# A maximum over rows on Trainium2: a first load of two rows from its own contiguous megabyte, with its own store, and the last two rows in alternating pieces

## The chip, the cores and the metric

One core of one Trainium2 chip. The metric is the device time of one execution in microseconds (us), lower is better. "Span" is the time from the first to the last instruction in the profile of one execution; the time is a little longer than the span. A transfer "lands" when the last of the 16 DMA engines has reported its share done.

## The reference

```python
batch, seq, dim = 32, 512, 1024
x = np.random.randn(batch, seq, dim).astype(np.float32)     # 67.11 MB
out = np.max(x, axis=-1)                                     # 16384 floats, 64 KB
```

x is 16384 rows of 1024 floats. The kernel treats it as 128 partitions of 128 rows. Below, "a row" is one row in each of the 128 partitions, so 512 KB; a load of 15 rows is 7.86 MB.

## The kernel before

The 128 rows are divided in blocks. In a block of S rows, partition p takes rows p*S to p*S+S-1 of the block, so each load brings a contiguous run per partition, and the results of a partition are S neighbouring floats of the output. Loads go through a ring of 46 rows. VectorE reduces each load; a few parts of late rows are reduced elsewhere (TensorE transposes, ScalarE copies, GpSimd reduces over partitions, TensorE turns the result back, VectorE merges). At the end the results of the two blocks are stored: the first block as 128 runs of 112 floats (448 bytes), in three stores, the second as 128 runs of 16 floats (64 bytes).

```python
BLOCKS = [
    [15, 15, 15, 14, 12, 11, 9, 8, 7, 6],     # 112 rows
    [4, 3, 2, 2, 1, 1, 1],                    # 14 rows, and two more in pieces
]
RING = 46
...
for sizes in BLOCKS:
    S = sum(sizes) + 2 * (sizes is BLOCKS[-1])
    xb = xf[first * P:(first + S) * P, :].rearrange("(p i) d -> p i d", p=P)
    dst = bass.AP(tensor=of.tensor, offset=of.offset + first * P, ap=[[S, P], [1, S]])
    views.append((dst, res[:, first:first + S]))
...                                           # loads and reduces
piece = ring[:, at, :D - K]                   # 689 columns of the last row but one
nc.sync.dma_start(out=piece, in_=xb[:, S - 2, :D - K])
...                                           # 671 columns across both rows, 688 of the last
for p, q in ((0, 48), (48, 96), (96, P)):
    store = nc.scalar.dma_start(out=views[0][0][p:q], in_=views[0][1][p:q])
    tc.add_manual_dep(store.ins, latest_row.ins.name, SYNC, reason="behind the loads")
nc.scalar.dma_start(out=views[1][0], in_=views[1][1])
```

## Time and profile before

| | before |
|---|---|
| time, median of 4 runs | 164.04 us (163.95 to 164.29) |
| span of the profiled run | 162.3 us |
| time less span | 1.8 us |
| load queue | 67.11 MB, 96.7% of the 16 engines' span |
| VectorE busy | 135.4 us, 83% |

The 15-row loads land at an even 1.209 us a row, the smaller ones at nearly that, and what follows the last landing is a reduce and a store. The list of DMA issues of the last microseconds (columns: number of issues, KB of each, median us from issue to landing):

```profile
out_dram<-res ACTq DMA_DIRECT2D x2, 21.0 KB, 1.5
out_dram<-res ACTq DMA_DIRECT2D x1, 14.0 KB, 1.5
out_dram<-res ACTq DMA_DIRECT2D x1, 8.0 KB, 1.4
```

### The profile page before, as it was taken

How to read it: one execution, taken by the hardware profiler on the slowest of the kernel's cores; microseconds unless marked ns; L12 is line 12 of the kernel's file. 1: busy time of each engine (PE TensorE's matmuls, PEld its weight loads, DVE VectorE, ACT ScalarE, POOL GpSimd, SP SyncE). 2: the span in 40 equal slices, each digit the busy share in tenths (PEclk: the TensorE clock that was granted, in tenths of full speed). 3: DMA queues.
4: the chain of work that ended last, by engine and by line, in shares of the span. 5: the costliest groups of instructions: out<-in, count | busy, mean ns of one | idle time of the engine just before them, and what ended most of it. 6: DMA issues, size and time to landing. Idle time of an engine off the chain costs nothing.

```text
span 162.3 us, 305 instructions
## 1 busy us (share of the span) xinstructions
PE 14.0 (9%) x76; PEld 12.0 (7%) x76; DVE 135.4 (83%) x35; ACT 6.3 (4%) x8; POOL 16.2 (10%) x11
## 2 busy tenths in 40 slices
PE   0000000000000000000000000000003010736540
PEld 0000000000000000000000000000002010725440
DVE  3000079995999779998999999999999999999994
ACT  3000000000000000000000000000001000222020
POOL 0000000000000000000000000000000500095970
DMA  7999699988999699999998998999999999999990
GB/s 242 485 485 454 273 485 485 485 379 348 485 485 485 285 410 452 452 452 388 497 472 371 433 455 355 436 436 420 509 396 445 452 395 396 440 411 423 405 379 18
DMA packets 3200, 67.18 MB, mean 414 GB/s; under 512 B 640, under 2 KB 640, under 8 KB 1408
## 3 DMA queue, kind: packets, MB, share of 16 engines
q1 hardware_dynamic: 2880, 67.11, 96.7%
q10 hardware_dynamic: 320, 0.07, 0.2%
HBM read 67.11 MB, written 0.07 MB: 414 GB/s over the span
## 4 chain that ended last, share of the span: by engine, by line
DVE 57%; DMA 36%; issue 5%; DVEq 0%
DVE res L168 52%; DMA ring<-in_x_dram 36%; DVE fetched L168 5%; DVEq L249 0%
## 5 line engine op out<-in xcount | busy, mean ns | idle before, releaser
L168 DVE TENSOR_REDUCE res<-ring 128x15 f32<-128x15360 f32 (+10 forms) x15 | 124.1, 8302 | 23.7 <-DMA ring<-in_x_dram 23.7
L143 POOL PARTITION_ALL_REDUCE top<-sb x7 | 16.0, 2330 | 141.8 <-ACT sb L141 141.8
L135 PE MATMUL ps<-ident,ring 128*128 128x128 f32 x38 | 9.3, 425 | 133.8 <-DMA ring<-in_x_dram 133.8
L135 PEld LDWEIGHTS ps<-ident,ring 128*128 128x128 f32 x38 | 7.5, 223 | 134.1 <-issue 127.8
L141 ACT COPY sb<-ps 128x768 f32<-128x768 f32 (+3 forms) x7 | 5.1, 739 | 150.2 <-PE ps L135 150.2
L168 DVE TENSOR_REDUCE fetched<-ring 128x2 f32<-128x1280 f32 (+3 forms) x5 | 8.5, 1699 | 0.0
L161 PE MATMUL fetched<-ident,top 1*128 1x1 f32 x38 | 4.8, 243 | 10.8 <-DVE fetched L168 7.3
L161 PEld LDWEIGHTS fetched<-ident,top 1*128 1x128 f32 x38 | 4.5, 213 | 12.5 <-issue 8.0
L168 DVE TENSOR_REDUCE res<-res 128x2 f32<-128x672 f32 (+1 forms) x2 | 1.7, 858 | 0.0
L141 ACT ACT_TABLE_LOAD x1 | 1.3, 1283 | 0.7 <-PEq L238 0.7
L83 DVE MEMSET ident<- 128x128 f32 x1 | 0.2, 165 | 0.8 <-PEq L238 0.8
L168 DVE TENSOR_REDUCE res<-fetched 128x2 f32<-128x8 f32 (+3 forms) x5 | 0.7, 158 | 0.0
L90 DVE TENSOR_SCALAR rowno<-rowno 32x1 f32<-32x1 f32 x3 | 0.4, 146 | 0.1
L85 DVE TENSOR_TENSOR_SCAN colno<-ident 128x128 f32<-128x128 f32 x1 | 0.4, 425 | 0.0
L92 DVE TENSOR_SCALAR ident<-colno,rowno 128x128 f32<-128x128 f32 x1 | 0.3, 285 | 0.0
L87 DVE STREAM_TRANSPOSE rowno<-colno 128x32 f32<-128x32 f32 x1 | 0.2, 213 | 0.0
L238 POOL MEMSET const-float32-0.0<- 128x1 f32 x1 | 0.1, 98 | 0.2 <-issue 0.2
L238 POOL MEMSET const-bfloat16-1.0<- 128x1 bf16 x1 | 0.1, 101 | 0.0
L238 POOL MEMSET const-uint8-127<- 128x1 uint8 x1 | 0.1, 101 | 0.0
L238 POOL MEMSET const-float32-1.0<- 128x1 f32 x1 | 0.1, 99 | 0.0
L84 DVE MEMSET rowno<- 128x32 f32 x1 | 0.1, 85 | 0.0
## 6 DMA issues: line engine op xcount, KB each, us to landing
ring<-in_x_dram SPq DMA_DIRECT2D x3, 7680.0 KB, 38.4
ring<-in_x_dram SPq DMA_DIRECT2D x1, 7168.0 KB, 37.0
ring<-in_x_dram SPq DMA_DIRECT2D x1, 6144.0 KB, 33.4
ring<-in_x_dram SPq DMA_DIRECT2D x1, 5632.0 KB, 28.6
ring<-in_x_dram SPq DMA_DIRECT2D x1, 4608.0 KB, 39.1
ring<-in_x_dram SPq DMA_DIRECT2D x1, 4096.0 KB, 33.3
ring<-in_x_dram SPq DMA_DIRECT2D x1, 3584.0 KB, 29.0
ring<-in_x_dram SPq DMA_DIRECT2D x1, 3072.0 KB, 35.9
```

The lines of the kernel that those rows point to most:

```text
L83: in_turn("DVE", nc.vector.memset(ident, 1.0))
L84: in_turn("DVE", nc.vector.memset(rowno, 0.0))
L85: in_turn("DVE", nc.vector.tensor_tensor_scan(out=colno, data0=ident, data1=ident, initial=-1.0, op0=ALU.add, op1=ALU.mult))
L87: in_turn("DVE", nc.vector.transpose(out=rowno, in_=colno[:, :32]))
L90: in_turn("DVE", nc.vector.tensor_scalar(out=part, in0=part, scalar1=float(q * 32), scalar2=None, op0=ALU.add))
L92: in_turn("DVE", nc.vector.tensor_scalar(out=ident, in0=colno, scalar1=rowno[:, 0:1], scalar2=None, op0=ALU.is_equal))
L135: in_turn("PE", nc.tensor.transpose(out=ps[:, k * P:(k + 1) * P], in_=rows(j)[:, loads[j][1] - m + r + i, c0 * P:(c0 + 1) * P], identity=i ...
L141: in_turn("ACT", nc.scalar.copy(out=sb[:, :W], in_=ps[:, :W]))
L143: in_turn("POOL", nc.gpsimd.partition_all_reduce(top[:, :W], sb[:, :W], P, bass_isa.ReduceOp.max))
L161: in_turn("PE", nc.tensor.transpose(out=share(j)[:, c0, r + i:r + i + 1], in_=tops[j, c][0:1, k * P:(k + 1) * P], identity=ident[0:1, 0:1],))
L168: return in_turn("DVE", nc.vector.reduce_max(out=out, in_=in_, axis=X))
L238: nc = _bacc.Bacc("TRN2", target_bir_lowering=False, num_devices=1)
```

## The change

The intent: VectorE should not wait 18.9 us for its first load, so the first load has 2 rows only. They are a block of their own, so that load reads one contiguous megabyte; a block has its own store. The last two rows come in four pieces in turn (first part of each row, then the rest), so the last reduce is shorter, and merges stand later in VectorE's order. The diff, cut to its core:

```diff
 BLOCKS = [
-    [15, 15, 15, 14, 12, 11, 9, 8, 7, 6],
-    [4, 3, 2, 2, 1, 1, 1],
+    [2],
+    [15, 9, 15, 14, 12, 10, 9, 9, 8, 6, 5],
+    [4, 3, 2, 1, 1, 1],
 ]
-RING = 46
-SHARED = {7: (2, 3), 9: (4, 4), 11: (3, 3), 13: (2, 3), 16: (1, 1)}
+RING = 47
+SHARED = {9: (1, 4), 10: (2, 4), 11: (2, 4), 12: (3, 2), 13: (2, 3), 14: (2, 3), 17: (1, 2)}
+PIECES = [(604, 420), (568, 456)]
+PLAN = """
+    d0 d1 d2 d3 d4 d5 d6 d7 d8 d9 t0 t1 p9 d10 b0 p10 t2 m9 d11 b1 p11 m10 d12 t3 p12 b2 m11
+    d13 t4 p13 b3 t5 p14 m12 d15 b4 d16 m13 p17 t6 f0 b5 f1 f2 b6 m14 f3 m17
+""".split()
...
-    ring = once.tile([P, RING, D], F32)
-    res = once.tile([P, MID + D - W], F32)
+    ring = once.tile([P, I + RING * D], F32)
+    res = ring[:, :I]
...
-    for p, q in ((0, 48), (48, 96), (96, P)):
-        store = nc.scalar.dma_start(out=views[0][0][p:q], in_=views[0][1][p:q])
-        tc.add_manual_dep(store.ins, latest_row.ins.name, SYNC, reason="behind the loads")
-    nc.scalar.dma_start(out=views[1][0], in_=views[1][1])
+    for dst, src in views[:-1]:
+        store = nc.scalar.dma_start(out=dst, in_=src)
+        tc.add_manual_dep(store.ins, behind.ins.name, SYNC, reason="behind the loads")
+    nc.scalar.dma_start(out=views[-1][0], in_=views[-1][1])
```

In PLAN, d is a direct reduce of a load, p the part of a shared load that VectorE keeps, t and b the way to the other engines and back, m a merge, f a reduce of a piece. The stores are now 128 runs of 2 floats (8 bytes), of 112 floats (448 bytes), and of 14 floats (56 bytes).

More of the change, by code (lines that the diff above doesn't have):

```diff
@@ L13 @@
 BLOCKS = [
-    [15, 15, 15, 14, 12, 11, 9, 8, 7, 6],
-    [4, 3, 2, 2, 1, 1, 1],
-]
-RING = 46
-SHARED = {7: (2, 3), 9: (4, 4), 11: (3, 3), 13: (2, 3), 16: (1, 1)}
-TENSOR = [
-    ("turn", 7, 0), ("back", 7, 0), ("turn", 9, 0), ("turn", 9, 1),
-    ("back", 9, 0), ("turn", 11, 0), ("turn", 11, 1), ("back", 9, 1),
-    ("turn", 13, 0), ("back", 11, 0), ("back", 11, 1), ("turn", 16, 0),
-    ("back", 13, 0), ("back", 16, 0),
-]
-MERGE = {8: (7,), 12: (9,), 15: (11,), 18: (13, 16)}
+    [2],
+    [15, 9, 15, 14, 12, 10, 9, 9, 8, 6, 5],
+    [4, 3, 2, 1, 1, 1],
+]
+RING = 47
[5 more added lines that the diff above has]
+""".split()
 NOSYNC = mybir.DependencyInfo(mybir.DependencyClass.NoSync, mybir.DependencyReason.DATA)
@@ L48 @@
     N, D = xf.shape
-    H = D // 2
     C = D // P
@@ L58 @@
     psmall = ctx.enter_context(tc.tile_pool(name="psmall", bufs=4, space=bass.MemoryType.PSUM))
-    ring = once.tile([P, RING, D], F32)
-    W = 336
-    K = W - 1
-    AT = I + 16
-    MID = AT + K + W + 17
-    res = once.tile([P, MID + D - W], F32)
+    ring = once.tile([P, I + RING * D], F32)
+    res = ring[:, :I]
     latest = {}
@@ L76, in in_turn, with maximum @@
         return inst
+    def maximum(out, in_):
+        return in_turn("DVE", nc.vector.reduce_max(out=out, in_=in_, axis=X))
     ident = once.tile([P, P], F32)
@@ L91 @@
             out=part, in0=part, scalar1=float(q * 32), scalar2=None, op0=ALU.add))
-    in_turn("DVE", nc.vector.tensor_scalar(
+    identity = in_turn("DVE", nc.vector.tensor_scalar(
         out=ident, in0=colno, scalar1=rowno[:, 0:1], scalar2=None, op0=ALU.is_equal))
     loads = []
+    views = []
+    last = len(PIECES)
     first = at = 0
-    views = []
     for sizes in BLOCKS:
-        S = sum(sizes) + 2 * (sizes is BLOCKS[-1])
+        S = sum(sizes) + last * (sizes is BLOCKS[-1])
         xb = xf[first * P:(first + S) * P, :].rearrange("(p i) d -> p i d", p=P)
@@ L111, with share, turn @@
     assert first == I
-    def chunks(j):
-        m, parts = SHARED[j]
+    shared = [SHARED.get(j, (0, C)) for j in range(len(loads))]
+    chunks = []
+    for j, (m, parts) in enumerate(shared):
         per = max(1, C // parts)
-        return [(r, min(per, m - r)) for r in range(0, m, per)]
+        chunks += [(j, r, min(per, m - r)) for r in range(0, m, per)]
     def rows(j):
         start, n, _, _ = loads[j]
-        return ring[:, start:start + n, :]
+        return ring[:, I + start * D:I + (start + n) * D].rearrange("p (i d) -> p i d", d=D)
     tops = {}
-    backs = {}
-    def turn(j, c):
-        m, parts = SHARED[j]
-        r, q = chunks(j)[c]
+    fetched = {}
+    def share(j):
+        m, parts = shared[j]
+        if j not in fetched:
+            got = psmall.tile([P, parts + (parts < C), m], F32)
+            fetched[j] = got
+        return fetched[j]
+    def turn(k):
+        j, r, q = chunks[k]
+        m, parts = shared[j]
         W = q * parts * P
@@ L132, in turn @@
         for i in range(q):
-            for c0 in range(parts):
-                k = i * parts + c0
+            for c in range(parts):
+                w = (i * parts + c) * P
                 in_turn("PE", nc.tensor.transpose(
-                    out=ps[:, k * P:(k + 1) * P],
-                    in_=rows(j)[:, loads[j][1] - m + r + i, c0 * P:(c0 + 1) * P],
+                    out=ps[:, w:w + P],
+                    in_=rows(j)[:, loads[j][1] - m + r + i, c * P:(c + 1) * P],
                     identity=ident,
@@ L144, in turn, with back @@
             top[:, :W], sb[:, :W], P, bass_isa.ReduceOp.max))
-        tops[j, c] = top
-    def share(j):
-        m, parts = SHARED[j]
-        if j not in backs:
-            fetched = psmall.tile([P, parts + (parts < C), m], F32)
-            backs[j] = fetched
-        return backs[j]
-    def back(j, c):
-        m, parts = SHARED[j]
-        r, q = chunks(j)[c]
+        tops[k] = top
+    def back(k):
+        j, r, q = chunks[k]
+        parts = shared[j][1]
         for i in range(q):
-            for c0 in range(parts):
-                k = i * parts + c0
+            for c in range(parts):
+                w = (i * parts + c) * P
@@ L161, in back @@
                 in_turn("PE", nc.tensor.transpose(
-                    out=share(j)[:, c0, r + i:r + i + 1],
-                    in_=tops[j, c][0:1, k * P:(k + 1) * P],
+                    out=share(j)[:, c, r + i:r + i + 1],
+                    in_=tops[k][0:1, w:w + P],
                     identity=ident[0:1, 0:1],
                 ))
-    def maximum(out, in_):
-        return in_turn("DVE", nc.vector.reduce_max(out=out, in_=in_, axis=X))
-    def merge(j):
-        for i in MERGE.get(j, ()):
-            _, k, _, c0 = loads[i]
-            q, _ = SHARED[i]
-            maximum(res[:, c0 + k - q:c0 + k], share(i).rearrange("p k m -> p m k"))
@@ L177, with direct, partial @@
-    issued = done = 0
-    todo = list(TENSOR)
-    for j in range(len(loads)):
-        while issued < len(loads) and issued < j + 3:
+    def direct(j):
+        _, n, _, col = loads[j]
+        k = n - shared[j][0]
+        maximum(res[:, col:col + k], rows(j)[:, :k, :])
+    def partial(j):
+        m, parts = shared[j]
+        maximum(share(j)[:, parts, :], rows(j)[:, loads[j][1] - m:, parts * P:])
+    def merge(j):
+        _, n, _, col = loads[j]
+        maximum(res[:, col + n - shared[j][0]:col + n], share(j).rearrange("p k m -> p m k"))
@@ new lines @@
+    at = at if at + last + 1 <= RING else 0
+    pieces = []
+    tail = []
+    room = I + at * D
+    for q in range(len(PIECES[0])):
+        for r, widths in enumerate(PIECES):
+            c, w = sum(widths[:q]), widths[q]
+            room = -(-(room + 1) // 16) * 16
+            pieces.append((ring[:, room:room + w], xb[:, S - last + r, c:c + w]))
+            if q:
+                tail[-last] = (ring[:, room - 1:room], tail[-last][1])
+            tail.append((res[:, I - last + r:I - last + r + 1],
+                         ring[:, room - (q > 0):room + w]))
+            room += w
@@ L181, with issue @@
+    assert room <= I + (at + last + 1) * D
+    readers = [0] * len(loads)
+    for step in PLAN:
+        if step[0] in "dp":
+            readers[int(step[1:])] += 1
+        elif step[0] == "t":
+            readers[chunks[int(step[1:])][0]] += 1
+    issued = 0
+    behind = None
+    def issue():
+        nonlocal issued
+        while issued < len(loads):
             start, n, src, _ = loads[issued]
-            held = any(s < start + n and start < s + k for s, k, _, _ in loads[j:issued])
@@ L183 @@
-            if held:
-                break
-            nc.sync.dma_start(out=rows(issued), in_=src)
+            if any(readers[j] and s < start + n and start < s + k
+                   for j, (s, k, _, _) in enumerate(loads[:issued])):
+                return
+            load = nc.sync.dma_start(out=rows(issued), in_=src)
             issued += 1
-        while todo and todo[0][1] < (j if todo[0][0] == "back" else issued):
-            what, i, c = todo.pop(0)
-            (turn if what == "turn" else back)(i, c)
@@ L190 @@
-        _, n, _, col = loads[j]
-        m, parts = SHARED.get(j, (0, 0))
-        if n > m:
-            maximum(res[:, col:col + n - m], rows(j)[:, :n - m, :])
-        if m and parts < C:
-            maximum(share(j)[:, parts, :], rows(j)[:, n - m:, parts * P:])
-        merge(j)
-    for what, i, c in todo:
-        assert what == "back"
-        back(i, c)
-    if at + 1 > RING:
-        at = 0
-    piece = ring[:, at, :D - K]
-    nc.sync.dma_start(out=piece, in_=xb[:, S - 2, :D - K])
-    pair = xb[:, S - 2:, :].rearrange("p i d -> p (i d)")
@@ L206 @@
-    nc.sync.dma_start(out=res[:, AT:AT + K + W], in_=pair[:, D - K:D + W])
-    nc.sync.dma_start(out=res[:, MID:], in_=pair[:, D + W:])
-    latest_row = maximum(res[:, AT - 1:AT], piece)
-    merge(len(loads))
-    maximum(
-        bass.AP(tensor=res.tensor, offset=res.offset + I - 2,
-                ap=[list(res.ap[0]), [MID - 1 - (I - 2), 2]]),
-        res[:, AT - 1:AT + K + W].rearrange("p (r k) -> p r k", r=2))
-    merge(len(loads) + 1)
-    maximum(res[:, I - 1:I], res[:, MID - 1:])
@@ L220 @@
-    for p, q in ((0, 48), (48, 96), (96, P)):
-        store = nc.scalar.dma_start(out=views[0][0][p:q], in_=views[0][1][p:q])
-        tc.add_manual_dep(store.ins, latest_row.ins.name, SYNC, reason="behind the loads")
-    nc.scalar.dma_start(out=views[1][0], in_=views[1][1])
+        if any(readers[j] and s < at + last + 1 and at < s + k for j, (s, k, _, _) in enumerate(loads)):
+            return
+        while pieces:
+            nc.sync.dma_start(out=pieces[0][0], in_=pieces[0][1])
+            pieces.pop(0)
@@ new lines @@
+    for step in PLAN:
+        issue()
+        kind, k = step[0], int(step[1:])
+        if kind in "dp":
+            (direct if kind == "d" else partial)(k)
+            readers[k] -= 1
+        elif kind == "t":
+            turn(k)
+            readers[chunks[k][0]] -= 1
+        elif kind == "b":
+            back(k)
+        elif kind == "m":
+            merge(k)
+        else:
+            inst = maximum(*tail[k])
+            if behind is None:
+                behind = inst
+    for dst, src in views[:-1]:
+        store = nc.scalar.dma_start(out=dst, in_=src)
+        tc.add_manual_dep(store.ins, behind.ins.name, SYNC, reason="behind the loads")
```

## The prediction

> **What bounds the kernel now.** I read the page's summary first, then VectorE's timeline, SyncE's timeline and waits, and last the helper engines near the end.
>
> The page (queue, kind: packets, MB, share of 16 engines' span):
>
> ```profile
> DVE  3000079995999779998999999999999999999994
> ...
> q1 hardware_dynamic: 2880, 67.11, 96.7%
> ...
> HBM read 67.11 MB, written 0.07 MB: 414 GB/s over the span
> ```
>
> VectorE is 83% busy but waits for loads; the load queue occupies the 16 engines for 96.7% of the span. 67.11 MB are all of x, and no version can read less. So the load stream is the first candidate, and the question is its pace. VectorE's timeline (start us, us, operation, idle before):
>
> ```profile
> 21.42 16.15 DVE L168 TENSOR_REDUCE res<-ring 128x15 f32<-128x15360 f32 x1 [18.91 <-DMA ring<-in_x_dram]
> 39.55 16.15 DVE L168 TENSOR_REDUCE res<-ring 128x15 f32<-128x15360 f32 x1 [1.98 <-DMA ring<-in_x_dram]
> 57.70 16.16 DVE L168 TENSOR_REDUCE res<-ring 128x15 f32<-128x15360 f32 x1 [1.99 <-DMA ring<-in_x_dram]
> 74.64 55.86 DVE L168 TENSOR_REDUCE res<-ring 128x14 f32<-128x14336 f32 x5 [0.79 <-DMA ring<-in_x_dram]
> ...
> 157.34 0.86 DVE L168 TENSOR_REDUCE res<-ring 128x1 f32<-128x689 f32 x1
> 158.24 0.85 DVE L168 TENSOR_REDUCE res<-res 128x2 f32<-128x672 f32 x1
> 159.01 0.22 DVE L168 TENSOR_REDUCE res<-fetched 128x2 f32<-128x8 f32 x2
> 159.15 0.86 DVE L168 TENSOR_REDUCE res<-res 128x1 f32<-128x689 f32 x1
> ```
>
> Each of the first starts just after its load has landed. 15-row loads (7.864 MB) land 18.13 to 18.15 us apart: 434 GB/s. The reduces take 1.077 us a row against 1.209 us of loading, so VectorE gains 0.13 us on the stream with every row; it loses its slack only because it first waits 18.9 us. From 74.64 on it never idles in this view, so at the end both limits nearly meet. SyncE's timeline shows when the last pieces are issued; its waits say what for:
>
> ```profile
> 138.93 0.33 SPq L204 DMA_DIRECT2D ring<-in_x_dram  x1
> 143.82 0.33 SPq L206 DMA_DIRECT2D res<-in_x_dram  x1
> 147.52 0.33 SPq L207 DMA_DIRECT2D res<-in_x_dram  x1
> ```
>
> ```profile
> SPq L204 <- DMA ring<-in_x_dram: 7.0, 1, 7.0
> SPq L206 <- DMA ring<-in_x_dram: 4.5, 1, 4.5
> SPq L207 <- DMA ring<-in_x_dram: 3.3, 1, 3.3
> ```
>
> Each issue waits for the DMA that used the same of eight completion semaphores before it, here the loads of 6, 4 and 3 rows, so 143.82 and 147.52 are landing times. 4 rows took 4.89 us, 3 rows 3.70, 15 rows 18.14, 14 rows 16.94 (57.70 to 74.64). One line fits all four: **1.204 us a row plus 0.08 us a load**. The piece of line 207 lands 11.5 us after its issue began (the view of DMA issues), at 159.0; the last reduce starts at 159.15. So the bound is the stream, never starved, then a tail of 3.3 us from the last landing to the end of the span (162.3). In the tail are the 0.86 us reduce, the last store, and the end of the program:
>
> ```profile
> 160.04 0.36 ACTq L223 DMA_DIRECT2D out_dram<-res  x1
> ```
>
> This store lands 1.4 us after its issue starts; some 0.9 us of closing waits follow.
>
> **What the Trainium skill says.** "DMA: Bandwidth & Descriptors", section Specifications, gives a fabric ceiling of 435 GB/s into SBUF and about 358 GB/s of HBM for a core. The trace agrees with the first (434 GB/s in the large loads) and exceeds the second; with one core running, 435 is the roof, so 67.11 MB cannot take under 154.3 us (an estimate from that page's figure). The same page, "Why a DMA increments its semaphore by 16 and not by 1", says that only the full count means that all data has landed; so the slowest of 16 engines sets each landing. The trace's landing records agree: for the first load the fifteenth engine reports at 21.14 us and the last at 21.39. "VectorE: DVE Perf Modes", "The perf-mode tier table", gives tensor_reduce no mode above one element a cycle; the trace agrees, 16155 ns for 15360 elements, 1.05 ns each. No page says that a contiguous first megabyte starts faster.
>
> **The change part by part.**
>
> *Small first load.* VectorE's first 18.9 us wait becomes about 3.3: the stream's effective start, 21.42 - 18.14 = 3.28, plus 2 x 1.204 + 0.08 puts the first landing at 5.77. VectorE then does 2.2 us of work and waits again, for the 15 rows, until 3.28 + 2.49 + 18.14 = 23.9. So VectorE is 2 rows ahead of where it would have been, but the stream has the same bytes to move. VectorE's slack is worth nothing unless its lag was the end. It was, by 159.15 - 159.0 = 0.15 us at most.
>
> *Count of loads.* 17 loads and 3 pieces become 18 and 4. One load more: +0.08 us. The old three pieces carry two rows (2 x 1.204 = 2.41 us); the last ordinary load lands at 3.28 + 126 x 1.204 + 17 x 0.08 = 156.34 (the transposes of that row do start at 156.45), so the pieces take 159.0 - 156.34 = 2.7 us, an overhead of 0.1 us each. One piece more: +0.1 us. The last landing moves from about 159.03 to **159.2**.
>
> *Ring.* I walked the new order: load 4 (14 rows) needs loads 0 and 1 reduced, at 40.1, while load 3 streams until about 52; load 5 needs load 2 (49.8) before 69; loads 6 and 7 need load 3 (69.1) before 84; load 9 needs load 5 (97.8) before 118. The last pieces wait for landings of loads 10 to 13 (135.4 to 150.1), with five rows still queued. At each point at least 10 us of data are queued. The stream isn't starved: 0 us.
>
> *The new tail.* Landings by the same line: load 13 at 150.05, 14 at 152.54, 15 to 17 at 153.82, 155.10 and 156.39; the pieces of 604, 568, 420 and 456 columns at 157.21, 157.98, 158.58 and 159.23. VectorE at 1.042 ns an element and 0.06 us from one start to the next: d12 146.4, p12 147.5, m11 149.97, d13 150.07, p13 151.2, p14 152.6, m12 153.98, d15 154.1, d16 155.2, m13 156.33, p17 156.43, f0 157.3, f1 158.0, f2 158.65, m14 159.15, f3 159.25. Every one is within 0.1 to 0.3 us of the landing that it needs: the plan is balanced. f3 reads 457 elements: 0.62 us to its end against 0.86 for 689: **-0.24 us**. But the merge m17 is now behind it, +0.1 us. VectorE ends at **159.95**, against 160.01 before.
>
> *Helpers.* The reductions handed to TensorE, ScalarE and GpSimd grow from 38 to 40 blocks of 128 columns, 0.28 us less for VectorE, already in the walk. The last one, of load 17, is what could be late:
>
> ```profile
> 156.45 0.45 PE L135 MATMUL ps<-ident,ring 128*128 128x128 f32 x1 [1.29 <-DMA ring<-in_x_dram]
> ...
> 157.65 0.95 PE L161 MATMUL fetched<-ident,top 1*128 1x1 f32 x7 [0.76 <-POOL top L143]
> ```
>
> Now two blocks: transposes done near 157.0, copy 157.45, GpSimd free from the one before at about 157.5, some 1.05 us for 256 columns (the earlier 768 took 2.50 us, 384 1.4, 128 0.7), back by 159.0. m17 wants it at 159.8: 0.8 us in hand. "Merges later" protects this; before, no merge made VectorE idle either.
>
> *Stores.* Three stores of the first block become one of 112 columns plus one of 2; both are issued behind f0, at about 158 and 158.5, before the last at 160. They lie beside the last reduces. 0 us.
>
> **Sum:** +0.08 +0.1 in the stream, -0.24 +0.1 in the last reduce and merge, about -0.1 for the lag of 0.15 that is gone: -0.06 us. Span 162.2; the time is 1.8 us above the span now (164.1 to 162.3), so **164.0 us**.
>
> **The rivals.** (1) *The tail slips.* Between the landings of load 17 and of the last piece, 2.84 us, VectorE has 2.8 us of work (p17 to m14). If starts cost 0.1 us instead of 0.06, or a merge waits for GpSimd, the end moves 0.3 to 0.8 us: 164.3 to 164.8. Against it: the old tail ran as tightly. (2) *The stream starts differently.* Data at full pace is reckoned from 3.28 although the first issue is at 0.72; with 8 KB packets from one megabyte this loss could shrink or grow by up to 0.5 us, and the engine that is 0.25 us late could be level: 163.4 to 164.5. The profile has no such start to compare. (3) *VectorE was the bound, and its early start pays.* The unbroken work from 74.64 speaks for it. If true, most of the 2 rows' early work would be a gain, about 2 us: 162. But the last two starts follow landings by 0.12 us, and the roof forbids it. (4) *Starvation:* a wait for a completion semaphore holds the issue long enough to empty the queue; 2 us or more, 166 or more. The walk shows no such place.
>
> **Range and chances.** Rivals 1 and 2 give most of the spread: **163.3 to 164.7**. Faster by over 2% needs 160.8, which would put the last landing at 155.7, a stream above the 434 GB/s seen: 1%. Slower by over 2%, 167.4, needs starvation: 2%. Within 2%: **97%**.
>
> **What would show it.** In the changed profile: first reduce at about 5.8 and the second at 23.9; the last f reduce starts at 159.1 to 159.4 right after its landing; the load queue's share stays at 96 to 97%; span 161.8 to 162.9. Right in mechanism: last landing within 0.3 us of before. It would be wrong if the first landings differ from 5.8 and 23.9 by over 0.5 us, if the loading pace in the middle leaves 1.209 us a row, or if f3 starts over 0.3 us after its landing.

## More of the kernel before

All runs told here were in the undisturbed state.

All four stores of the kernel before land about 1.5 us after their issue.

## The result

The changed kernel took 165.73 us (median of 4 runs, 165.63 to 166.21) against 164.04. The ratio is 1.0106, with a 95% interval of 1.0093 to 1.012. (Every ratio here is from fast runs of the same rounds, and not quite the ratio of the medians.) The output is correct. The rise of 1.7 us is clear of noise and lies outside the predicted range; at 1.1% it is within the 2% that the prediction gave 97%.

The page of the changed kernel, the lines that answer to those of before:

```profile
span 164.0 us, 325 instructions
...
DVE  3500019999992999899999999999999999999990
...
q1 hardware_dynamic: 3168, 67.11, 95.6%
q10 hardware_dynamic: 432, 0.07, 0.2%
```

VectorE now has a little work in the second of the 40 slices, then waits. The same bytes are moved. VectorE's timeline of the changed kernel:

```profile
5.58 2.29 DVE L75 TENSOR_REDUCE ring<-ring 128x2 f32<-128x2048 f32 x1 [3.07 <-DMA ring<-in_x_dram]
23.83 25.81 DVE L75 TENSOR_REDUCE ring<-ring 128x15 f32<-128x15360 f32 x2 [15.96 <-DMA ring<-in_x_dram]
52.89 16.15 DVE L75 TENSOR_REDUCE ring<-ring 128x15 f32<-128x15360 f32 x1 [3.25 <-DMA ring<-in_x_dram]
69.83 48.33 DVE L75 TENSOR_REDUCE ring<-ring 128x14 f32<-128x14336 f32 x4 [0.78 <-DMA ring<-in_x_dram]
...
157.25 1.92 DVE L75 TENSOR_REDUCE ring<-ring 128x1 f32<-128x604 f32 x3
159.09 0.16 DVE L75 TENSOR_REDUCE ring<-got 128x2 f32<-128x8 f32 x1
159.16 0.62 DVE L75 TENSOR_REDUCE ring<-ring 128x1 f32<-128x457 f32 x1
159.70 0.15 DVE L75 TENSOR_REDUCE ring<-got 128x1 f32<-128x3 f32 x1
```

This is the predicted walk within 0.2 us: first reduce 5.58 (5.8 predicted), second 23.83 (23.9), last reduce 159.16 (159.25), end of VectorE 159.85 (159.95). VectorE ends 0.16 us **earlier** than in the kernel before (160.01). And still the span ends 1.7 us later. What lies between is the stores. ScalarE's queue issues them on time:

```profile
158.06 0.86 ACTq L237 DMA_DIRECT2D out_dram<-ring  x2
159.88 0.34 ACTq L239 DMA_DIRECT2D out_dram<-ring  x1
```

But the list of DMA issues of the last microseconds of the changed kernel shows that they land late:

```profile
out_dram<-ring ACTq DMA_DIRECT2D x1, 56.0 KB, 4.5
out_dram<-ring ACTq DMA_DIRECT2D x1, 1.0 KB, 3.9
out_dram<-ring ACTq DMA_DIRECT2D x1, 7.0 KB, 3.2
```

(SyncE's waits at the end of the program don't measure this: its longest wait for a store is 4.1 us here and 0.8 before, but also 4.1 in blocks_3_stores and 5.1 in before_more_loads, two runs told below whose stores all land in 1.4 to 1.5 us.) In the trace's packet records the 8-byte packets of the smallest store are done at 159.13, but its sixteen landing records come in from 159.77 to 162.00. The two other stores land right behind it, 162.15 to 162.94 and 162.72 to 163.12.

There is a second part. The four runs of the changed kernel have spans of 164.0, 163.5, 163.5 and 163.4 us, a mean of 163.6, with times 2.23 us longer than the spans on average. In all runs of the kernel before whose spans are on record, the time is 1.78 us longer than the span on average. So about 0.45 us of the rise do not stand in the span at all.

### The profile page after: what moved, and what is told of

Same layout as the page of the kernel before. It is cut to its first block, busy times and chain, and to the rows that moved or that the text cites. A ratio compares the mean times of both kernels' runs of the same rounds, so it can differ in the third digit from the quotient of the medians.

```text
span 164.0 us, 325 instructions
## 1 busy us (share of the span) xinstructions
PE 15.3 (9%) x80; PEld 12.3 (8%) x80; DVE 135.6 (83%) x42; ACT 6.7 (4%) x8; POOL 17.0 (10%) x11
## 3 DMA queue, kind: packets, MB, share of 16 engines
q1 hardware_dynamic: 3168, 67.11, 95.6%
## 4 chain that ended last, share of the span: by engine, by line
DMA 55%; DVE 40%; issue 2%; SPq 0%; DVEq 0%
DMA ring<-in_x_dram 55%; DVE ring L75 37%; DVE got L75 3%; SPq L210 0%; DVEq L264 0%
## 5 line engine op out<-in xcount | busy, mean ns | idle before, releaser
L75 DVE TENSOR_REDUCE ring<-ring 128x1 f32<-128x1024 f32 (+13 forms) x20 | 125.0, 6281 | 23.3 <-DMA ring<-in_x_dram 23.2
L147 POOL PARTITION_ALL_REDUCE top<-sb x7 | 16.8, 2399 | 141.5 <-ACT sb L145 141.5
L139 PE MATMUL ps<-ident,ring 128*128 128x128 f32 x40 | 10.2, 425 | 142.0 <-DMA ring<-in_x_dram 138.0
L75 DVE TENSOR_REDUCE got<-ring 128x2 f32<-128x1024 f32 (+4 forms) x7 | 9.6, 1371 | 0.0
L157 PE MATMUL got<-ident,top 1*128 1x1 f32 x40 | 5.4, 244 | 1.9 <-POOL top L147 1.9
L157 PEld LDWEIGHTS got<-ident,top 1*128 1x128 f32 x40 | 4.8, 212 | 4.2 <-POOL top L147 3.5
L75 DVE TENSOR_REDUCE ring<-got 128x2 f32<-128x10 f32 (+4 forms) x7 | 1.1, 156 | 0.0
```

The lines of the kernel that those rows point to most:

```text
L75: return in_turn("DVE", nc.vector.reduce_max(out=out, in_=in_, axis=X))
L139: in_turn("PE", nc.tensor.transpose(out=ps[:, w:w + P], in_=rows(j)[:, loads[j][1] - m + r + i, c * P:(c + 1) * P], identity=ident,))
L147: in_turn("POOL", nc.gpsimd.partition_all_reduce(top[:, :W], sb[:, :W], P, bass_isa.ReduceOp.max))
L157: in_turn("PE", nc.tensor.transpose(out=share(j)[:, c, r + i:r + i + 1], in_=tops[k][0:1, w:w + P], identity=ident[0:1, 0:1],))
```

## The experiments

Four theories of the stores were set against each other: (A) the 8-byte store is confirmed late and holds up what lands after it; (B) the last store is slow, as its runs are now 56 bytes and not 64; (C) the one store of 112 columns, formerly three, is slow; and, after the first runs, (D) what counts is whether neighbouring runs share a 64-byte line of memory. For the part outside the span, the rivals are counts of instructions, the number of stores, the place of the results and the size of the ring.

All edits are to the changed kernel ("after") or to the kernel before. Ratios are against runs of the kernel before in the same rounds.

| run | from | time, us | ratio | mean span | time less span |
|---|---|---|---|---|---|
| no_small_store | after | 164.22 | 1.0015 | 162.0 | 2.2 |
| early_small_store | after | 165.83 | 1.0114 | 163.7 | 2.2 |
| early_apart | after | 164.27 | 1.0012 | 162.0 | 2.2 |
| last_2_of_2 | before | 167.23 | 1.0207 | 165.5 | 1.8 |
| last_2_of_8 | before | 165.12 | 1.0052 | 163.3 | 1.8 |
| last_2_of_16 | before | 164.16 | 1.0006 | 162.3 | 1.8 |
| last_14_of_14 | before | 164.59 | 1.0040 | 162.9 | 1.8 |
| last_14_of_16 | before | 164.10 | 1.0005 | 162.3 | 1.8 |
| last_8_of_8 | before | 164.04 | 1.0004 | 162.3 | 1.8 |
| blocks_of_64B | after | 164.32 | 1.0019 | 162.1 | 2.2 |
| blocks_38 | after | 164.57 | 1.0029 | 162.4 | 2.2 |
| blocks_3_stores | after | 164.48 | 1.0015 | 162.4 | 2.2 |
| blocks_own_res | after | 164.30 | 1.0006 | 162.1 | 2.2 |
| blocks_ring46 | after | 164.12 | 1.0009 | 161.9 | 2.2 |
| before_padded | before | 164.05 | 1.0002 | 162.3 | 1.8 |
| before_pe40 | before | 165.00 | 1.0055 | 163.2 | 1.8 |
| before_more_loads | before | 164.36 | 1.0017 | 162.6 | 1.8 |
| before_1_store | before | 164.30 | 1.0005 | 162.5 | 1.8 |

### The small store taken away, or moved

```diff
-    for dst, src in views[:-1]:
+    for dst, src in views[1:-1]:          # no_small_store
```

> The changed kernel without the store of the first block (2 columns, 128 rows of 8 bytes); its 256 results are left unwritten on purpose, so the output is wrong. In the changed profile that store's landing records run from 159.77 to 162.00 us although its packets were done at 159.13, and the two later stores land behind it at 162.94 and 163.12. Theory A (the 8-byte store is confirmed late and holds up what lands after it): the last store lands about 1.4 us after its issue, as before, span about 162.1, time 163.9 to 164.1, 1% under the changed kernel. Theory B (the last store itself is slow, since its rows are now 56 bytes instead of 64): landing of the last store stays near 3.2 us after issue, time 165.4 to 165.8. Theory C (the one store of 112 columns, formerly three, is slow): it still lands over 3 us after issue, time 165 or more.

Measured: 164.22 us, span 162.0. The two remaining stores, of the same shapes as in the changed kernel, land at once:

```profile
out_dram<-ring ACTq DMA_DIRECT2D x1, 56.0 KB, 1.6
out_dram<-ring ACTq DMA_DIRECT2D x1, 7.0 KB, 1.4
```

This settles A against B and C for the changed kernel: the 56-byte runs and the single store of 112 columns are not slow there; they only landed behind the small store. The small store is worth 163.6 - 162.0 = 1.6 us of span. Without it, the rest of the change is 0.2 us **better** in the span than the kernel before (162.23 on average in those rounds).

```diff
             (direct if kind == "d" else partial)(k)
             readers[k] -= 1
+            if step == "d0":                # early_small_store
+                nc.scalar.dma_start(out=views[0][0], in_=views[0][1])
...
-    for dst, src in views[:-1]:
+    for dst, src in views[1:-1]:
```

> The changed kernel with the 2-column store issued as soon as the first reduce is done (about 8 us) instead of at the end. All results correct. Theory A: its slow landing is hidden beside the loads; time 163.9 to 164.2, and its own landing is still 3 us or more after issue. If A is right but the store also delays loads on its engines, the landing of the load after it moves by up to 2 us and the time stays between 164.2 and 165.7. Theories B and C: 165.4 to 165.8, unchanged.

Measured: 165.83 us; nothing was hidden. VectorE's timeline without the small store, first, and with it issued at 8.0 us:

```profile
23.66 25.81 DVE L75 TENSOR_REDUCE ring<-ring 128x15 f32<-128x15360 f32 x2 [15.83 <-DMA ring<-in_x_dram]
52.74 16.15 DVE L75 TENSOR_REDUCE ring<-ring 128x15 f32<-128x15360 f32 x1 [3.27 <-DMA ring<-in_x_dram]
```

```profile
24.12 25.81 DVE L75 TENSOR_REDUCE ring<-ring 128x15 f32<-128x15360 f32 x2 [16.19 <-DMA ring<-in_x_dram]
54.22 16.16 DVE L75 TENSOR_REDUCE ring<-ring 128x15 f32<-128x15360 f32 x1 [4.29 <-DMA ring<-in_x_dram]
```

The load that feeds the reduce at 52.74 lands 1.48 us later, and everything behind it keeps that delay: the last piece lands at 160.34 instead of 158.87. The DMA view of the ten microseconds from 22 to 32 shows the hole, first without the small store, then with it:

```profile
DMA packets 128, 4.13 MB, mean 413 GB/s; under 512 B 16, under 2 KB 16, under 8 KB 16
```

```profile
DMA packets 184, 3.54 MB, mean 354 GB/s; under 512 B 88, under 2 KB 88, under 8 KB 88
```

0.59 MB less were moved, 1.4 us at 434 GB/s. So A in its first form fails too: it is not a late confirmation that could hide beside other work. In both places tried the store costs about the same, 1.6 us of span at the end and 1.5 us of the load stream here, where the engines are the bound. In the packet records, 61 KB packets that alternate with single 8-byte packets still take some 2270 ns up to 22 us; packets of 36 KB, 1364 ns elsewhere, take up to 2574 where they start between 24.5 and 28.5 us.

### The store by itself, and how its runs lie in memory

The kernel before, with only its last store altered in width and pitch:

```diff
-    nc.scalar.dma_start(out=views[1][0], in_=views[1][1])
+    nc.scalar.dma_start(
+        out=bass.AP(tensor=of.tensor, offset=of.offset + 112 * P, ap=[[PITCH, P], [1, COLS]]),
+        in_=res[:, I - COLS:I])
```

> The kernel before with only its last store altered: 2 of the 16 columns, rows of 8 bytes packed into 1 KB (wrong on purpose). This is the disputed store by itself, with nothing of the change's other parts. Theory A: it lands 3.5 to 4 us after issue instead of 1.4, with the engines' reports spread over about 2.2 us; the time rises by 2.2 to 2.6 us to 166.2 to 166.7. Theory B and C: it lands like the others, 164.0.

> The kernel before with only its last store altered: 14 of the 16 columns, rows of 56 bytes packed one after another, so rows share 64-byte lines (the output is wrong on purpose). Theory A: landing about 1.4 to 1.6 us after issue, time as before, 164.0. Theory B: landing over 2.5 us after issue, time 165 or more.

> The kernel before, last store of 14 columns written at a pitch of 16: 56-byte rows, each alone in a 64-byte line (wrong on purpose). Packed 56-byte rows cost 0.6 us of time. If sharing of a line by neighbouring rows is what costs, this run is as before, 164.0, landing 1.4 us after issue. If a row that fills only part of a line is what costs, 164.4 to 164.8.

> The kernel before, last store of 2 columns written at a pitch of 16: 8-byte rows, each alone in its 64-byte line (wrong on purpose). Packed 8-byte rows cost 3.2 us. If sharing is what costs: back to 164.0 to 164.3. If being a part of a line costs: as much as the 56-byte rows at this pitch, or as the packed 8-byte rows if shortness costs: 167.

> The kernel before, last store of 2 columns at a pitch of 8: 8-byte rows, two in each 64-byte line (wrong on purpose). Eight in a line cost 3.2 us, one in a line nothing. If the piece of memory that may not be shared is 64 bytes: a cost between, 0.3 to 1.5 us, since each line has one conflict instead of seven. If it is 32 bytes: 164.0 to 164.2, as before.

> The kernel before, last store of 8 columns packed: rows of 32 bytes, two in each 64-byte line (wrong on purpose). Two rows of 8 bytes in a line cost 0.9 us of time. If the sharing of a 64-byte line costs whatever the rows' length: 164.6 to 165.2. If rows that are whole pieces of 32 bytes are free: 164.0 to 164.2.

The last store in the list of DMA issues, in this order: 2 of 2, 2 of 8, 2 of 16, 14 of 14, 14 of 16, 8 of 8.

```profile
out_dram<-res ACTq DMA_DIRECT2D x1, 1.0 KB, 4.4
```

```profile
out_dram<-res ACTq DMA_DIRECT2D x1, 1.0 KB, 2.4
```

```profile
out_dram<-res ACTq DMA_DIRECT2D x1, 1.0 KB, 1.6
```

```profile
out_dram<-res ACTq DMA_DIRECT2D x1, 7.0 KB, 2.5
```

```profile
out_dram<-res ACTq DMA_DIRECT2D x1, 7.0 KB, 1.6
```

```profile
out_dram<-res ACTq DMA_DIRECT2D x1, 4.0 KB, 1.4
```

Two of these runs had fitted no theory of the first round: the packed 8-byte runs cost more than A allowed (167.23 us against 166.7 at most), and the packed 56-byte runs fell between A and B (164.59). Hence D and the other four.

The same 128 runs of 8 bytes land 4.4 us after issue if eight share a 64-byte line, 2.4 if two do, and 1.6 if each has a line to itself. A short run as such costs no more than 0.2 us; sharing costs. That is theory D, and the line must be larger than 32 bytes, as runs 32 bytes apart still pay. The 56-byte runs agree: packed 2.5, apart 1.6. The last run adds a limit: runs of a full 32 bytes, two to a line, cost nothing. So what pays in these six runs is a run that fills a 32-byte piece only in part **and** has a neighbour in its 64-byte line.

One thing does not fit and stays open. Packed 56-byte runs cost 0.6 us here, but nothing in no_small_store, where the same shape lies 1024 bytes further on and the store before it had landed 1.1 us earlier instead of 0.3 (nor in early_small_store and early_apart, where they land in 1.4 us too). Which of these matters was not tried, so the condition above is not the whole of it.

```diff
-                nc.scalar.dma_start(out=views[0][0], in_=views[0][1])
+                nc.scalar.dma_start(out=bass.AP(tensor=of.tensor, offset=of.offset + 2 * P,
+                                                ap=[[16, P], [1, 2]]), in_=views[0][1])   # early_apart
...
-    for dst, src in views[1:-1]:
+    for dst, src in []:
```

> The changed kernel with its 2-column store early (as in the run of the early store, which stayed at 165.8 us because all later landings moved by 1.5 us), but its 8-byte rows written 64 bytes apart, each alone in its line; the 112-column store, whose place that takes, is left out (it hid beside the last reduces; the output is wrong on purpose). If rows of a few bytes sharing a line are what holds up the engines, the loads behind it land as in the run without the small store (last piece at 158.9) and the time is 164.2. If any 128 short writes amid loads hold them up, 165.5 to 165.9.

Measured: 164.27 us, span 162.0. The reduce that stood at 54.22 with packed runs is back, and so are the bytes of the window from 22 to 32 us:

```profile
52.81 16.15 DVE L75 TENSOR_REDUCE ring<-ring 128x15 f32<-128x15360 f32 x1 [3.23 <-DMA ring<-in_x_dram]
```

```profile
DMA packets 201, 4.13 MB, mean 413 GB/s; under 512 B 89, under 2 KB 89, under 8 KB 89
```

The same number of 8-byte packets amid the loads, each alone in its line, delays the loads by 0.1 us at most (52.81 against 52.74). (This run also leaves out the store of 112 columns at the end, which is hidden in any case; the loads' landings, which decide it, come long before.)

### The change without short runs

```diff
 BLOCKS = [
-    [2],
-    [15, 9, 15, 14, 12, 10, 9, 9, 8, 6, 5],
-    [4, 3, 2, 1, 1, 1],
+    [2, 15, 9, 15, 14, 12, 10, 9, 9, 8, 6, 3],     # blocks_of_64B: runs of 448 and 64 bytes
+    [2, 4, 3, 2, 1, 1, 1],
 ]
```

SHARED and PLAN are renumbered for the load of 5 rows that became 3 and 2.

> The changed kernel with blocks of 112 and 16 rows again, as before: the first load still brings 2 rows, but from the block of 112, so no 8-byte store exists and the last store has 64-byte rows; one load of 5 rows is cut into 3 and 2 (19 loads and 4 pieces). All results correct. If the stores are the whole cost: last store lands 1.4 us after issue, last landing of a piece at 159.0 to 159.2, span 162.0 to 162.4, and the time is 163.8 to 164.2 if the time outside the span is 1.8 us as for the kernel before, or 164.2 to 164.5 if it is the 2.2 us seen for the changed kernel and two of its relatives (then something other than the stores costs 0.4 us outside the profile). If anything else of the change costs time inside the span: 165 or more.

Measured: 164.32 us, correct, span 162.1, with the last reduce at 159.10 and the two stores landing in 1.6 and 1.4 us. The stores are the whole of the cost inside the span, and the first load need not be contiguous: here it lies at a pitch of 448 KB and lands at 5.49 us, against 5.56 in the changed kernel. The rest of the change gains some 0.1 us of span (means of 5 and 9 runs; single spans of the kernel before differ by 0.3 us), and 0.45 us are lost outside it.

> The aligned version (blocks of 112 and 16) without its last hand-over to the other engines: the last one-row load is reduced by VectorE alone, so 38 blocks of 128 columns go to TensorE as in the kernel before, and no merge stands behind the last reduce. Inside the span: VectorE has 0.27 us more to do in the last 3 us and 0.2 us less of merges: span 162.0 to 162.3. Outside the span: if the 0.4 us come from TensorE's number of instructions (179 records instead of 169), they vanish and the time is 163.8 to 164.1; else 164.2 to 164.5.

Measured: 164.57 us, span 162.4. Without the last hand-over, VectorE's last reduce starts at 159.37 instead of 159.10, its 0.27 us as expected; span and time came out just above the ranges given. Outside the span 2.2 us as before, so TensorE's instructions are not the reason.

### Parts of the change in the kernel before

> The kernel before with its three loads of 15 rows cut in two (2 and 13, 8 and 7, 8 and 7): 23 loads on SyncE, first reduce at 5.6 us. Outside the span 2.2 us if SyncE's instructions make the difference, else 1.8. Span: three loads at 0.08 us each, minus nothing for the early start: 162.4 to 162.7; if VectorE's early start is worth something in itself, less than 162.2.

The edit also lets loads be issued up to six ahead instead of three, and renumbers the helpers' loads.

Measured: 164.36 us, span 162.6. VectorE's timeline has the early start and gains nothing by it:

```profile
5.67 2.29 DVE L168 TENSOR_REDUCE res<-ring 128x2 f32<-128x2048 f32 x1 [3.16 <-DMA ring<-in_x_dram]
21.37 46.26 DVE L168 TENSOR_REDUCE res<-ring 128x13 f32<-128x13312 f32 x5 [13.41 <-DMA ring<-in_x_dram]
74.75 55.87 DVE L168 TENSOR_REDUCE res<-ring 128x14 f32<-128x14336 f32 x5 [7.12 <-DMA ring<-in_x_dram]
```

VectorE waits 7.12 us for the load at 74.75, where it waited 0.79 in the kernel before. The work done early turns into a longer wait. The span rises by 0.3 us, about the predicted 0.24 of three more loads, though in two runs only, and the interval of the ratio (0.9997 to 1.0037) just includes 1. This also tells against the prediction's third rival, that VectorE was the bound.

> The kernel before, handing 40 instead of 38 blocks to TensorE (the last row three blocks instead of one). If TensorE's number of instructions makes the 0.4 us outside the span, outside is 2.2 us here; else 1.8. The span may rise by up to 0.5 us, because the last merge comes later.

Measured: 165.00 us, span 163.2, outside 1.8. With three blocks of the last row handed over and the merges where they were, VectorE waits for TensorE before the merge that stands ahead of its last reduce:

```profile
159.88 0.16 DVE L168 TENSOR_REDUCE res<-fetched 128x1 f32<-128x4 f32 x1 [0.83 <-PE fetched L161]
```

So a larger hand-over needs later merges, as the change has them.

### The 0.45 us outside the span

> The kernel before with 20 more tiny VectorE instructions in its first wait, where they cost nothing on the path. The changed kernel and its relatives have 0.4 us more outside the span than the kernel before, and 19 or 20 more instructions. If the instruction count is the reason: span 162.3 as before, time 164.4. If not: 164.0.

> The kernel before with one store of 112 columns in place of three. If the number of stores makes the 0.4 us: span 162.3, time 164.5. If not: 164.0 to 164.1.

> The aligned version (blocks of 112 and 16) with its store of 112 columns cut in three again (48, 48 and 32 rows), so four stores as in the kernel before. If the number of stores makes the 0.4 us outside the span, they vanish: span 162.1, time 163.8 to 164.0, below the kernel before by 0.1 us. If not: 164.3.

> The aligned version with the results in a tile of their own and not in front of the ring's. If the layout or the store's source makes the 0.4 us outside the span, outside is 1.8 us; else 2.2, time 164.3.

> The aligned version with a ring of 46 rows instead of 47. Every load gets the same place as with 47, so the instructions are the same; only the tile is 4 KB a partition smaller, as in the kernel before. If the size of the tile makes the 0.45 us outside the span, outside is 1.8 us and the time 163.9; else 2.2 us and 164.3, and the cause of the 0.45 us stays open.

All five went against their candidate: outside stayed 1.8 us in the two relatives of the kernel before and 2.2 in the three of the changed kernel, to within 0.05 us. With before_more_loads (23 loads on SyncE, still 1.8) and before_pe40 and blocks_38 (TensorE), this excludes, each taken alone, the instruction counts of VectorE, TensorE and SyncE, the number of stores, the tile that holds the results, and the ring's size. What makes it **stays open**; the profile does not reach outside the span.

No version beat the kernel before. The best, blocks_ring46, has a span 0.3 us shorter and a time of 164.12 against 163.99, a ratio whose interval (0.9989 to 1.0029) includes 1.

## Why the prediction was wrong

**The bound: right.** The stream was said to set the end, and it does: last landing 159.01 in the changed kernel (159.2 predicted), no starvation, and an early start worth nothing (before_more_loads).

**Ring, new tail, helpers: right.** All starts of VectorE are within 0.2 us of the walk, and the last reduce and its merge give the -0.24 and +0.1 us of the sum. (The walk's landings of loads 13 to 17 stand 0.03 us below the prediction's own line, which changes nothing.)

**Count of loads and lag: two small misses that cancel.** The last landing moved by 0.03 us (158.98 to 159.01), not by 0.18; ten profiles with the loads of the kernel before have it between 158.85 and 159.10, so a term of this size can't be read off one profile. And the lag of 0.15 us from the last landing to the last reduce, counted as gone, is still there (159.01 to 159.16). That the sum of -0.06 us is near the -0.16 us of VectorE's end is thus partly luck. Without the small store the span is 0.2 us shorter than before.

**Stores: wrong, and this is the step that failed.** The prediction said of the three new stores that they lie beside the last reduces, "0 us". It placed their issues, at 158 and 158.5 and before the last at 160, and took the landing, 1.4 us in the one store that it looked at, for given, whatever the shape. The store of 8-byte runs takes 3.9 us to land and holds up the two behind it: 1.6 us of span by its removal (163.6 to 162.0). The term was 0 and should have been 1.6. Nor was it one of the rivals; the list of what would prove the prediction wrong looked at VectorE and the loads and not at the landing of the last store, which ends the program. By its own test of the mechanism, a last landing within 0.3 us of before, it would have passed (0.03); of its other signs, the span (164.0, not 161.8 to 162.9) and the load queue's share (95.6%, not 96 to 97) went against it.

The view that should have raised the question is the list of DMA issues with its landing times. It has landings for the two old shapes alone, 448 and 64 bytes a run, both whole numbers of 64-byte lines; the new shapes of 8 and 56 bytes are not, and nothing on record told how they land. "DMA: Bandwidth & Descriptors", section Specifications, which the prediction quotes for its ceiling, also names 512 bytes as the least transfer for the full rate, with a read-modify-write below; no run here shows such a thing. It would have misled: runs of 448, 64 and 32 bytes and even lone runs of 8 land in 1.4 to 1.6 us. But it points to run length as something to ask about. The slow landing itself agrees with "Perfetto Trace Analysis", section DMA Instruction — HWDGE (DVE, Sync), which warns that the wait for the confirmation of the last write can be "a surprisingly long delay especially when the write target is HBM"; here 2.9 us from the last packet to the last landing record (159.13 to 162.00). The last store of the kernel before, to the same memory, took 0.4 us for it (161.10 to 161.47), so the warning doesn't tell which store will be slow.

**Time from span: wrong by 0.45 us.** The prediction added the 1.8 us of the kernel before to its span. For every relative of the changed kernel it is 2.2. Together: -0.2 + 1.6 + 0.45 = 1.85 us, for a measured rise of 1.75 (means of 165.83 against 164.08 in the same rounds; the terms come from other rounds).

That the mechanism of the slow store is a read-modify-write of a shared line is only argued. What is shown is that the cost goes when each run has a line to itself, or fills 32 bytes.

## What to carry to other kernels

Look at where each run of a store lies in memory, not only at bytes and issues: here 8-byte runs that shared a 64-byte line with their neighbours held up the DMA engines, and since these were the bound, moving the store earlier hid nothing. Stores of runs of 32, 64 and 448 bytes landed in 1.4 to 1.6 us. Divide work so that a partition's results are whole lines. And when the stream of loads is the bound, an idle engine at the start is no loss; judge a change there by when the last byte and the last store land.

## What the Trainium skill lacked or had wrong

- "DMA: Bandwidth & Descriptors" has no word on runs of a store that share a line of memory without overlapping (only "Collectives: The Full Stack" has a line on 32-byte alignment, for its buffers). 128 runs of 8 bytes, written to HBM, land 4.4 us after issue at eight to a 64-byte line, 2.4 at two, 1.6 at one; runs of 32 bytes at two to a line land in 1.4.
- The same page's 512 bytes as the least size for full rate isn't contradicted (a packet of 448 bytes took 25 ns, 18 GB/s an engine, one of 61 KB 2267 ns, 27 GB/s). But its read-modify-write below 512 bytes does not tell which small stores land late here: runs of 64 and 448 bytes landed in 1.4 and 1.5 us, and lone runs of 8 bytes in 1.6.
- No page says that a store of 1 KB from a core to HBM can hold up its loads on the same engines ("DMA: Bandwidth & Descriptors" has stalled writes that stall other queues for transfers between cores alone): with the 8-byte runs packed, the loads behind came 1.5 us late; with them 64 bytes apart, by 0.1 us at most.
- No page explains a part of the time outside the span that differs by kernel: 1.8 us for every relative of one kernel, 2.2 for every relative of the other.
